# Interleaving the high and low parts of stationary matmul operands in a split-precision transformer kernel

## The chip, the cores and the metric

The kernel runs on one core of one Trainium2 chip. The metric is the device time of one execution in microseconds. Before the change three runs took 1825.13 us in the median, from 1824.33 to 1829.41. TensorE multiplies matrices, VectorE and ScalarE work element by element, GpSimd does some element work, and SyncE starts almost all DMA transfers.

## The reference

A small network of four layers is applied to 256 tokens of 1024 channels (and, in the first layer, to 256 context tokens besides). What matters here is that nearly all of its time goes into products of activations with weights:

```python
ql = pl[..., :D] ...                       # pl = u_lat @ w          (attention projections)
y_lat = swa(...) @ swa_wo[j]
h_lat = h_lat + ga2 * squared_relu_mlp(..., mlp_w1[i], mlp_w2[i])   # 1024 -> 4096 -> 1024
u = (xn @ w_in)                            # state-space mixer, then gelu(y) @ w_glu
val, gate = split(xn @ w_up); (silu(conv(gate)) * val) @ w_down     # 1024 -> 2 x 2816 -> 1024
```

Layer 0 attends in a neighbourhood, layer 1 in a sliding window, then come a state-space mixer with a gated MLP and a stick-breaking attention with another gated MLP. All is in 32-bit floating point.

## The kernel before

**Products of three terms.** TensorE multiplies the type float32r several times faster than float32, but keeps fewer bits. The kernel therefore writes each operand as high + low, both float32r, and makes each product of three: high x high, high x low, low x high. Every matmul has a stationary operand (`lhsT`, 128 columns, loaded ahead of it) and a moving one (`rhs`, 256 or 512 columns here). There are two forms.

- `mm_w` (lines 290 to 296): channels on the output's partitions, weights stationary, activations moving. Used for output projections, MLPs and the gated unit.
- `mm_x` (lines 298 to 304): tokens on the output's partitions, activations stationary, weights moving, 256 columns. Used for queries, keys, values and the input of the state-space mixer. A weight of 256 columns takes eight contraction tiles by four token tiles in layer 0 (12 such weights) and for the keys and values of layer 1 (2), and by two elsewhere (4 + 4 + 12): 14 x 32 + 20 x 16 = 768 of each of the three lines.

```python
294     T.matmul(ps, lhsT=a, rhs=xh[k][:, s0:s1], start=first, stop=False)       # mm_w: a, b = high, low weights
295     T.matmul(ps, lhsT=a, rhs=xl[k][:, s0:s1], start=False, stop=False)
296     T.matmul(ps, lhsT=b, rhs=xh[k][:, s0:s1], start=False, stop=last_)
302     T.matmul(ps, lhsT=xh[k][:, t0:t0 + 128], rhs=a, start=first, stop=False) # mm_x
303     T.matmul(ps, lhsT=xh[k][:, t0:t0 + 128], rhs=b, start=False, stop=False)
304     T.matmul(ps, lhsT=xl[k][:, t0:t0 + 128], rhs=a, start=False, stop=last_)
```

**Weights** (class `Weights`, lines 244 to 280). A part of at most 1024 elements per partition, that is eight column tiles of 128, comes by DMA from SyncE's queue into a `raw` tile. `split` (line 228) then makes `whi` with ScalarE (line 111, a copy that rounds) and `wlo` with VectorE (line 114, raw - whi). Each has its own tile of [128, 1024] from a pool of four buffers (line 862), and of five from layer 1's end on (line 1405): `wtile` (line 234) hands them out in turn. With `by_k`, used for `mm_x`, a part holds half the contraction with all 256 columns; without it, used for `mm_w`, one column tile of 128 with the whole contraction (or half of it). In `mm_w` a part of eight column tiles feeds 24 matmuls. With 512 tokens these stream 512 columns, with 256 tokens 256. The gated MLP opens two parts at a time, 48 matmuls of 256 columns.

**Activations.** `new_x` (line 486) makes tiles `xh0..7` and `xl0..7`, [128, 512] in the layers 0 and 1 and [128, 256] later; `normed` (line 470) and `gained` (line 465) fill them, high with ScalarE and low with VectorE. Hidden values and attention outputs lie in tiles `oh0..7` and `ol0..7` of another pool, [128, 512], made with the same function; the mixer's output `gh`, `gl` lies in four of each and moves in the 16 x 8 = 128 products per line of the gated unit. The state-space mixer takes its tokens in another order (`turned`, line 1452): there the elements of one instruction are written 128 bytes apart.

**The order of the work.** The program order is written out by hand. SyncE's queue starts loads in that order, each as soon as its buffer is free. In the attention stages `run_chains` (line 848) mixes scores, softmax and weighted sums of earlier heads with the projections of the next ones. Elsewhere products follow one another without a break, and each column tile's result is taken out of PSUM by VectorE or ScalarE while the next is made.

**Other users of the same memory.** While the program starts, the memory of `xh`, `xl` holds input rows and half tiles of conditioning weights (`stage`, line 872: 512 columns each). During the state-space mixer, `spare_w` (line 1428) lends idle `whi` and `wlo` tiles, in turns, to matrices that come back from DRAM.

Of the kernel before, what the change touches and what calls it, by code (L numbers as in the profile page):

```python
# [8 lines left out]
F32 = mybir.dt.float32  # L9
F32R = mybir.dt.float32r  # L10
# [7 lines left out]
KT = 8  # L18
# [67 lines left out]
def _build(ctx, tc, I, out, dbg):  # L86
# [10 lines left out]
    last = [None]  # L97
# [74 lines left out]
    def vector_loads(va, cc):  # L172
        """loads of the small vectors, most urgent first."""
# [58 lines left out]
    wpool, n_w = [], {}  # L232

    def wtile(tag, name, dt=F32R):
        i = n_w[tag] = n_w.get(tag, -1) + 1
        n = sum(b for _, b in wpool)
        p = wpool[0][0] if i % n < wpool[0][1] else wpool[1][0]
        return p.tile([128, 1024], dt, tag=tag, name=name)

    def w_pool(name, bufs):  # L240
        wpool.append((ctx.enter_context(tc.tile_pool(name=name, bufs=bufs)), bufs))
        n_w.clear()

    class Weights:
        """src: dram view [128, kt, n] or [128, kt, n / 128, 128]; parts of at most 1024 elements."""

        def __init__(self, src, by_k=False):
# [8 lines left out]
            for k0, k1, c0, c1 in spans:  # L256
# [12 lines left out]
                hi = wtile("whi", "whi")[:, 0:m]  # L269
                lo = wtile("wlo", "wlo")[:, 0:m]  # L270
# [14 lines left out]
    def wpairs(w, s, c0):  # L285
        """two column tiles of 128, one in each of two neighbouring blocks of s columns."""
        b = w.rearrange("(k p) (b n) -> p k b n", p=128, n=s)
        return b[:, :, c0 // s:c0 // s + 2, c0 % s:c0 % s + 128]

    def mm_w(ps, w, c0, x, k, s0, s1, first, last_):  # L290
        """channel-major product, one contraction tile: weights stationary."""
# [6 lines left out]
    def mm_x(ps, w, c0, c1, x, k, t0, first, last_):  # L298
        """token-major product, one contraction tile: activations stationary."""
# [6 lines left out]
    def gemm_w(tiles, x, nk, s0, s1, evac, lead):  # L306
        """tiles: list of callables giving (weights, column, psum view, key); the first `lead` of them go
        through the contraction together, so that they can start before all of x is there."""
# [10 lines left out]
    class Early:  # L319
        """the first two column tiles of a product, begun while its last contraction tiles are still missing."""  # L320
# [78 lines left out]
    def square_sum(n, pooled, view=lambda v: v, late=KT - 2):  # L399
        """tiles whose columns sum, over the partitions, to those of h * h."""  # L400
# [20 lines left out]
    def rstd_rows(n, pooled=6, late=KT - 2):  # L421
        """1 / rms of every token, a quarter of them on each block of 32 partitions."""
# [19 lines left out]
    def rstd(n, pooled=6, late=KT - 2, tag="x"):  # L442
        """1 / rms of every token, on all partitions; left in PSUM."""
        return spread_cols(rstd_rows(n, pooled, late), n, tag)

    def rstd_cols(view=lambda v: v, pooled=6):
        """1 / rms of every token, tokens on partitions: [128, 2]; view gives the order of the tokens."""
# [11 lines left out]
    def gained(x, gain, view=lambda v: v):  # L459
        """x = gain * h, for products that are scaled by the tokens' 1 / rms afterwards."""  # L460
# [5 lines left out]
    def normed(x, r, n, gain, shift=None):  # L466
        """gain(k, v), shift(k, v): columns for contraction tile k and stream v."""
# [15 lines left out]
    def new_x(pool, tag, n):  # L483
        return [[pool.tile([128, n], F32R, tag=f"{tag}{p}{k}", name=f"{tag}{p}{k}") for k in range(KT)]
                for p in "hl"]
# [7 lines left out]
    def rsqrt(y, ss, n, pool):  # L493
        """y = 1 / sqrt(ss / 64 + eps), by a bit estimate and three Newton steps."""
# [10 lines left out]
    def head_scale(views, pool, scale=(None, None)):  # L505
        """1 / rms of every head of token-major products [128, 256] in PSUM, times a scale of the tokens."""
# [11 lines left out]
    def head_norm(views, pool, scale=(None, None)):  # L518
        """per-head normalisation of token-major products [128, 256]; views in PSUM."""
# [10 lines left out]
    def stack_q(o, q):  # L530
        """heads of q, token-major [128, n, 64], as blocks (high, low) of 128 columns."""
# [3 lines left out]
    def stack_k(oh, ol, k):  # L535
        """heads of k as blocks (high, high) and (low, low): with those of q, two products make the whole q k."""
# [12 lines left out]
    def cmul(o, a, b, t, conj=False, e=None):  # L549
        """o = a * b (pairs of real and imaginary views); conj: a * conj(b)."""  # L550
# [41 lines left out]
    class S5:  # L592
        """operators of the state space layer: e = a^s b, k = c a^t b, f = c a^t, and the phases of a^8t."""

        def __init__(self, pp, loads):
# [43 lines left out]
            # input matrix: ((a - 1) / lam) * b  # L639
# [32 lines left out]
        def c(self):  # L672
            pp, ct, ci, dr = self.pp, self.ct, self.ci, self.dr
            # output matrix, transposed: states onto partitions
# [101 lines left out]
        def phases(self, fp, hf):  # L776
            """powers 1..32 of exp(8 i theta), and |a|^8 with a zero where a new group starts."""
# [21 lines left out]
        def f(self, fp, i):  # L799
            """state-to-output matrices, a sixteenth of the groups: real(c a s) needs (re, -im) of c a."""  # L800
# [17 lines left out]
    def softmax_rows(ps, n, at, idn, tail=None):  # L818
        """rows of ps [128, n] -> unnormalised weights and idn scaled by the rows' 1/sum."""
# [28 lines left out]
    def run_chains(chains, lag):  # L848
        """chains: list of (score, probs, [finish of a group]); every group is two chains long.
        score() -> state, probs(state) -> transposed weights, finish([both])."""  # L850
# [13 lines left out]
    # ================ start ================  # L864
    w_pool("wsp", 4)
    with ExitStack() as sa:
# [5 lines left out]
        def stage(p, i):  # L872
# [957 lines left out]
```

## Time and profile before

| what | value |
|---|---|
| median of three runs | 1825.13 us (1824.33 to 1829.41) |
| span of the profiled execution | 1823.7 us |
| matmuls / weight loads (TensorE) | 95% / 84% of the span |
| VectorE, ScalarE, GpSimd | 65%, 43%, 26% |
| DMA engines, mean share | 52% |
| bytes moved | 286.68 MB |
| granted TensorE clock, mean | 0.980 |

The profiled execution's own time is given by its span, from the first to the last instruction; what lies around it isn't listed apart, and the span is 1.4 us below the median. How to read it: the busy share of TensorE is a modelled one, since matmuls overlap, and what a matmul costs in a row of them is the distance of their starts. In names such as `g<-xh,whi` the output comes first, then the moving operand, then the stationary one. PE stands for matmuls, PEld for loads of the stationary operand, DVE for VectorE, ACT for ScalarE, SP for SyncE. A clock of 1.00 is 2.4 GHz.

### The profile page before, as it was taken

Reading aid. Unit: us, or ns where it says so; the run is one execution under the profiler, and the core shown is the slowest. Engines: PE = TensorE matmul, PEld = TensorE weight load, DVE = VectorE, ACT = ScalarE, POOL = GpSimd, SP = SyncE. Lnnn points to the kernel's source line nnn. Section 1 sums busy time; section 2 is a strip of 40 time slices with the busy share of each in tenths; the row PEclk is TensorE's granted clock in tenths of the full one; section 3 lists DMA queues with packets and bytes.
Section 4 is the critical chain, followed back from the end, with each engine's and each line's share of the span. In section 5 each row is a group of like instructions: output and inputs, shape, how many; then the busy total and the mean of one; then the engine's idle time right before and its main releaser. Section 6 shows DMA issues by size and latency. Waiting matters only on the chain. (4 is left out here: it accounts for less than half of the span.)

```text
span 1823.7 us, 34377 instructions
## 1 busy us (share of the span) xinstructions
PE 1738.8 (95%) x13449; PEld 1537.9 (84%) x13449; DVE 1183.4 (65%) x2508; ACT 790.0 (43%) x1446; POOL 473.1 (26%) x633
## 2 busy tenths in 40 slices
PE   5899999999999999999999999998999999999999
PEld 3478888877777777888878999987899999889998
DVE  8556776775635434346986656768576788958674
ACT  4344444442413222223654545545444465535453
POOL 5311211115789300030102000202331332324130
PEclk8899999999999999999999999998999999999999
DMA  8565454325566655332215566688558564435852
GB/s 221 172 175 155 147 173 122 106 86 162 170 212 219 184 170 162 93 93 81 59 36 146 155 189 186 193 303 235 142 153 231 152 218 131 127 93 167 228 156 88
DMA packets 441045, 286.68 MB, mean 157 GB/s; under 512 B 50450, under 2 KB 418610, under 8 KB 440882
## 3 DMA queue, kind: packets, MB, share of 16 engines
q1 hardware_dynamic: 439122, 278.70, 52.4%
q0 software_dynamic: 1760, 5.77, 0.8%
q8 instruction: 106, 1.74, 0.4%
q14 instruction: 57, 0.47, 0.1%
HBM read 271.48 MB, written 17.15 MB: 158 GB/s over the span
## 5 line engine op out<-in xcount | busy, mean ns | idle before, releaser
L111 ACT ACTIVATE whi<-raw 128x1024 fp32r<-128x1024 f32 (+2 forms) x388 | 389.8, 1013 | 482.2 <-PE g L295 352.3
L114 DVE TENSOR_TENSOR wlo<-raw,whi 128x1024 fp32r<-128x1024 f32 (+2 forms) x388 | 466.4, 1207 | 189.8 <-ACT whi L111 186.7
L296 PE MATMUL g<-xh,wlo 128*128 128x256 f32 (+1 forms) x1216 | 375.2, 309 | 5.5 <-DVE wlo L114 5.2
L294 PE MATMUL g<-xh,whi 128*128 128x256 f32 (+1 forms) x1216 | 375.2, 310 | 1.3 <-ACT xh L111 1.2
L295 PE MATMUL g<-xl,whi 128*128 128x256 f32 (+1 forms) x1216 | 374.6, 308 | 0.0
L294 PE MATMUL g<-oh,whi 128*128 128x256 f32 (+1 forms) x1056 | 332.1, 315 | 3.3 <-DVE hc L117 1.4
L296 PE MATMUL g<-oh,wlo 128*128 128x256 f32 (+1 forms) x1056 | 331.0, 314 | 0.0
L295 PE MATMUL g<-ol,whi 128*128 128x256 f32 (+1 forms) x1056 | 330.8, 313 | 0.0
L296 PEld LDWEIGHTS g<-xh,wlo 128*128 128x128 f32 x1216 | 235.2, 193 | 17.9 <-DVE wlo L114 7.4
L294 PEld LDWEIGHTS g<-xh,whi 128*128 128x128 f32 x1216 | 234.7, 193 | 16.4 <-ACT whi L111 3.1
L295 PEld LDWEIGHTS g<-xl,whi 128*128 128x128 f32 x1216 | 235.3, 193 | 9.7
L294 PEld LDWEIGHTS g<-oh,whi 128*128 128x128 f32 x1056 | 198.3, 188 | 23.6 <-issue 3.9
L295 PEld LDWEIGHTS g<-ol,whi 128*128 128x128 f32 x1056 | 198.3, 188 | 15.3 <-issue 1.1
L296 PEld LDWEIGHTS g<-oh,wlo 128*128 128x128 f32 x1056 | 198.3, 188 | 14.5 <-issue 0.2
L302 PE MATMUL g<-whi,xh 128*128 128x256 f32 x560 | 166.9, 298 | 3.8 <-ACT xh L111 2.8
L303 PE MATMUL g<-wlo,xh 128*128 128x256 f32 x560 | 161.1, 288 | 0.6 <-DVE wlo L114 0.6
L304 PE MATMUL g<-whi,xl 128*128 128x256 f32 x560 | 160.5, 288 | 0.1
L117 DVE SCALAR_TENSOR_TENSOR h<-g,mods,h 128x256 f32<-128x256 f32 x64 | 30.8, 482 | 141.5 <-PE g L296 141.5
L302 PEld LDWEIGHTS g<-whi,xh 128*128 128x128 f32 x560 | 108.6, 194 | 13.3 <-issue 8.5
L303 PEld LDWEIGHTS g<-wlo,xh 128*128 128x128 f32 x560 | 108.8, 194 | 2.2 <-DVE wlo L114 1.7
L304 PEld LDWEIGHTS g<-whi,xl 128*128 128x128 f32 x560 | 108.1, 194 | 0.5 <-DVE xl L117 0.3
L111 ACT ACTIVATE oh<-t 128x256 fp32r<-128x256 f32 (+1 forms) x108 | 51.3, 482 | 125.5 <-DVE t L114 125.5
(300 smaller groups left out, 2943.3 us busy)
## 6 DMA issues: line engine op xcount, KB each, us to landing
raw<-mlp_w SPq DMA_DIRECT2D x128, 512.0 KB, 4.6
ada<-ada_w SPq DMA_DIRECT2D x88, 512.0 KB, 5.4
raw<-ffn_w_up SPq DMA_DIRECT2D x88, 512.0 KB, 5.2
raw<-ffn_w_down SPq DMA_DIRECT2D x32, 384.0 KB, 3.6
raw<-ffn_w_down SPq DMA_DIRECT2D x32, 320.0 KB
raw<-na_wqkv SPq DMA_DIRECT2D x32, 256.0 KB, 4.4
raw<-a_w_glu SPq DMA_DIRECT2D x16, 512.0 KB, 7.9
raw<-w_kv SPq DMA_DIRECT2D x16, 512.0 KB, 4.5
```

What stands on the lines that cost most here:

```text
L111: last[0] = A.activation(out=o, in_=i, func=f, **kw)
L114: (e or V).tensor_tensor(out=o, in0=a, in1=b, op=op)
L117: V.scalar_tensor_tensor(out=o, in0=a, scalar=s, in1=b, op0=op0, op1=op1)
L294: T.matmul(ps, lhsT=a, rhs=xh[k][:, s0:s1], start=first, stop=False)
L295: T.matmul(ps, lhsT=a, rhs=xl[k][:, s0:s1], start=False, stop=False)
L296: T.matmul(ps, lhsT=b, rhs=xh[k][:, s0:s1], start=False, stop=last_)
L302: T.matmul(ps, lhsT=xh[k][:, t0:t0 + 128], rhs=a, start=first, stop=False)
L303: T.matmul(ps, lhsT=xh[k][:, t0:t0 + 128], rhs=b, start=False, stop=False)
L304: T.matmul(ps, lhsT=xl[k][:, t0:t0 + 128], rhs=a, start=False, stop=last_)
```

## The change

The high and low parts of an operand now share one tile. Where the operand is stationary they are interleaved, element by element: high at even places, low at odd ones, so that each is read and written with a step of two elements (eight bytes). Where it moves, they lie one after the other, each contiguous. Weights are paired unless `by_k`; activations are paired where `mm_x` uses them (`True` below) and not where `mm_w` does. Tiles `oh`, `ol`, `gh`, `gl` stay as they were. The weight pool hands out tiles of [128, 2048], the same number of them, and the staging and spare tiles follow: staging tiles are 1024 wide, so the conditioning weights that went into two half tiles come with one DMA each, and two spare tiles are the halves of one.

```diff
-    def wtile(tag, name, dt=F32R):
-        i = n_w[tag] = n_w.get(tag, -1) + 1
-        n = sum(b for _, b in wpool)
-        p = wpool[0][0] if i % n < wpool[0][1] else wpool[1][0]
-        return p.tile([128, 1024], dt, tag=tag, name=name)
+    def wtile(name, dt=F32R):
+        n_w[0] += 1
+        p = wpool[0][0] if n_w[0] % sum(b for _, b in wpool) < wpool[0][1] else wpool[1][0]
+        return p.tile([128, 2048], dt, tag="w", name=name)
...
+    def two(t, n, paired):
+
+        if paired:
+            v = t.rearrange("p (n c) -> p c n", c=2)
+            return v[:, 0, 0:n], v[:, 1, 0:n]
+        return t[:, 0:n], t[:, n:2 * n]
...
-                hi = wtile("whi", "whi")[:, 0:m]
-                lo = wtile("wlo", "wlo")[:, 0:m]
+                hi, lo = two(wtile("w")[:, 0:2 * m], m, not by_k)
                 split(hi, lo, r)
...
-    def new_x(pool, tag, n):
-        return [[pool.tile([128, n], F32R, tag=f"{tag}{p}{k}", name=f"{tag}{p}{k}") for k in range(KT)]
-                for p in "hl"]
+    def new_o():
+        return [[actp.tile([128, 512], F32R, tag=f"o{p}{k}", name=f"o{p}{k}") for k in range(KT)] for p in "hl"]
+
+    def new_x(pool, tag, n, paired):
+
+        return list(zip(*[two(pool.tile([128, 2 * n], F32R, tag=f"{tag}{k}", name=f"{tag}{k}"), n, paired)
+                          for k in range(KT)]))
...
-        def stage(p, i):
-            return xa.tile([128, 512], F32, tag=f"x{p}{i}", name=f"st{p}{i}")
-
+        def stage(i):
+            return xa.tile([128, 1024], F32, tag=f"x{i}", name=f"st{i}")
...
-            halves = lambda k: [stage("l", 2 * (k // 2) + j) for j in range(2)] if k % 2 else None
+            halves = lambda k: [stage(4 + k // 2)] if k % 2 else None
...
-            x = new_x(xa, "x", 512)
+            x = new_x(xa, "x", 512, True)
...
-            x = new_x(xa, "x", 512)
+            x = new_x(xa, "x", 512, False)
             mod_norm(x, 0, 3, 512)
...
+        halves = []
+
         def spare_w():
-            """tiles of the pool of weight parts, which idles meanwhile."""
-            return wtile("whi" if n_w["whi"] == n_w["wlo"] else "wlo", "sw", F32)
+
+            if not halves:
+                t = wtile("sw", F32)
+                halves.extend((t[:, 1024:2048], t[:, 0:1024]))
+            return halves.pop()
...
-        x = new_x(xb, "x", 256)
+        x = new_x(xb, "x", 256, True)
         turned = lambda v: v.rearrange("p (t c) -> p c t", t=8)
...
-        x_ = new_x(xb, "x", 256)
+        x_ = new_x(xb, "x", 256, False)
...
-        xk = new_x(xb, "x", 256)
-        xq = new_x(ac, "xq", 256)
+        xk = new_x(xb, "x", 256, True)
+        xq = new_x(ac, "xq", 256, True)
```

The matmuls of lines 294 to 296 and 302 to 304 are not edited; only the views that they get are others. The rest of the diff takes comments away or passes the new arguments on.

## Rows read from the trace of the kernel before

**Rows 1.** The page, part 1: busy us, share of the span, instructions.

```profile
PE 1738.8 (95%) x13449; PEld 1537.9 (84%) x13449; DVE 1183.4 (65%) x2508; ACT 790.0 (43%) x1446; POOL 473.1 (26%) x633
```

**Rows 2.** Waits: us in total, times, longest us.

```profile
ACT whi L111 <- PE g L295: 352.3, 153, 8.7
...
PE g L296 <- DVE wlo L114: 5.8, 7, 1.9
```

**Rows 3.** Timeline of PE (start us, us), first and last of four unbroken sequences.

```profile
1439.76 0.28 PE L296 MATMUL g<-xh,wlo 128*128 128x256 f32 x1
...
1441.92 0.28 PE L296 MATMUL g<-xh,wlo 128*128 128x256 f32 x1
...
1081.79 0.28 PE L294 MATMUL g<-oh,whi 128*128 128x256 f32 x1
...
1083.83 0.28 PE L294 MATMUL g<-oh,whi 128*128 128x256 f32 x1
...
469.64 0.39 PE L296 MATMUL g<-xh,wlo 128*128 128x512 f32 x1
...
471.68 0.39 PE L296 MATMUL g<-xh,wlo 128*128 128x512 f32 x1
...
411.80 0.39 PE L296 MATMUL g<-oh,wlo 128*128 128x512 f32 x1
...
413.89 0.39 PE L296 MATMUL g<-oh,wlo 128*128 128x512 f32 x1
```

**Rows 4.** Windows, gated MLP: us; PE, PEld, DVE, ACT, POOL busy; PEclk, DMA share, GB/s.

```profile
1400.00:1455.00 55.00, 55.00 (x460) 55.00 (x459) 41.20 (x66) 26.16 (x37) 19.02 (x19) 1.00 0.59 169
```

**Rows 5.** Timeline of the weight loads (PEld).

```profile
1439.76 0.19 PEld L294 LDWEIGHTS g<-xh,whi 128*128 128x128 f32 x1
```

**Rows 6.** Lines, shapes apart: busy us, mean ns, idle before; L294, L302.

```profile
L294 PE MATMUL g<-xh,whi 128*128 128x256 f32 x960 | 274.6, 287 | 1.2 <-ACT xh L111 1.2
...
L294 PE MATMUL g<-oh,whi 128*128 128x256 f32 x736 | 204.0, 278 | 1.2 <-DVE h L117 0.7 <-ACT oh L111 0.5
...
L302 PE MATMUL g<-whi,xh 128*128 128x256 f32 x560 | 166.9, 298 | 3.8 <-ACT xh L111 2.8 <-DVE h L114 1.0
...
L294 PE MATMUL g<-oh,whi 128*128 128x512 f32 x320 | 128.1, 401 | 2.1 <-DVE hc L117 1.4 <-ACT oh L111 0.7
...
L294 PE MATMUL g<-xh,whi 128*128 128x512 f32 x256 | 100.6, 395 | 0.1
```

**Rows 7.** Timeline of PE, float32 products (two passes each).

```profile
145.82 1.05 PE L839 MATMUL pt<-dg,p 128*128 128x128 f32 x8
...
1550.87 0.60 PE L1721 MATMUL z<-kT,qz 128*128 128x256 f32 x2
1551.30 0.27 PE L1742 MATMUL pt<-cst,be 128*128 128x128 f32 x1
```

**Rows 8.** Splits by shape, then wider steps: ACT's in the timeline, DVE's by shape.

```profile
L111 ACT ACTIVATE whi<-raw 128x1024 fp32r<-128x1024 f32 x324 | 340.4, 1057 | 451.7 <-PE g L295 325.0 <-issue 38.5 <-PE g L304 34.3
...
L114 DVE TENSOR_TENSOR wlo<-raw,whi 128x1024 fp32r<-128x1024 f32 x324 | 409.8, 1268 | 172.1 <-ACT whi L111 169.1
...
1153.11 0.78 ACT L111 ACTIVATE xh<-h,vt 128x256 fp32r<-128x256 f32 x1
...
1280.34 0.51 ACT L111 ACTIVATE xh<-h,vt 128x256 fp32r<-128x256 f32 x1
...
L114 DVE TENSOR_TENSOR gl<-x,gh 128x128 fp32r<-128x128 f32 x16 | 6.0, 396 | 2.6 <-ACT gh L111 2.6
...
L114 DVE TENSOR_TENSOR qn<-g,ri 128x128 f32<-128x128 f32 x32 | 8.9, 279 | 0.0
```

**Rows 9.** Waits of PE for the staged conditioning weights.

```profile
PE x L360 <- DMA stl<-ada_w: 1.1, 1, 1.1
```

**Rows 10.** Timeline of PE, float32r transposes of 128 columns.

```profile
299.92 0.23 PE L1013 MATMUL pt<-idr,sp 128*128 128x128 f32 x1
...
300.39 0.62 PE L1013 MATMUL pt<-idr,sp 128*128 128x128 f32 x6
```

More of the change, by code (lines that the diff above doesn't have):

```diff
@@ L230, in split @@
         tt(o_lo, x, o_hi.bitcast(F32), SUB)
-    wpool, n_w = [], {}
-    def wtile(tag, name, dt=F32R):
-        i = n_w[tag] = n_w.get(tag, -1) + 1
-        n = sum(b for _, b in wpool)
-        p = wpool[0][0] if i % n < wpool[0][1] else wpool[1][0]
-        return p.tile([128, 1024], dt, tag=tag, name=name)
+    wpool, n_w = [], [-1]
+    def wtile(name, dt=F32R):
+        n_w[0] += 1
+        p = wpool[0][0] if n_w[0] % sum(b for _, b in wpool) < wpool[0][1] else wpool[1][0]
+        return p.tile([128, 2048], dt, tag="w", name=name)
     def w_pool(name, bufs):
         wpool.append((ctx.enter_context(tc.tile_pool(name=name, bufs=bufs)), bufs))
-        n_w.clear()
+        n_w[0] = -1
+    def two(t, n, paired):
[3 more added lines that the diff above has]
+        return t[:, 0:n], t[:, n:2 * n]
     class Weights:
@@ L894, in _build @@
                 for t in range(2):
-                    r = [stage("h", len(xt) * 2 + j) for j in range(2)]
+                    r = stage(len(xt))
                     for j in range(2):
                         xloads.append(lambda r=r, nm=nm, t=t, j=j: dma(
-                            out=r[j], in_=I[nm][0, t * 128:(t + 1) * 128, 512 * j:512 * j + 512]))
+                            out=r[:, 512 * j:512 * j + 512],
+                            in_=I[nm][0, t * 128:(t + 1) * 128, 512 * j:512 * j + 512]))
                     xt.append(r)
-            halves = lambda k: [stage("l", 2 * (k // 2) + j) for j in range(2)] if k % 2 else None
+            halves = lambda k: [stage(4 + k // 2)] if k % 2 else None
             ada_q = ada_steps(0, 0, halves) + ada_steps(0, 1, halves)
@@ L920, in _build @@
                 for t in range(4):
-                    T.transpose(ps[:, t * 128:(t + 1) * 128], xt[t][k // 4][:, (k % 4) * 128:(k % 4) * 128 + 128], ident)
+                    T.transpose(ps[:, t * 128:(t + 1) * 128], xt[t][:, k * 128:k * 128 + 128], ident)
                 act(h[k], ps[:, 0:256], AF.Copy)
@@ L1159, in mlp @@
         def mlp(l, ntok, x_, after=None):
-            hid = new_x(actp, "o", 512)
+            hid = new_o()
             per = 512 // ntok
@@ L1200, in _build @@
             dump("h0", 512)
-            x = new_x(xa, "x", 512)
+            x = new_x(xa, "x", 512, True)
             mod_norm(x, 1, 0, 512)
             mark("norm1")
-        oT = new_x(actp, "o", 512)
+        oT = new_o()
         with ExitStack() as s0:
@@ L1375, in _build @@
             rawp[0] = ctx.enter_context(tc.tile_pool(name="rawb", bufs=8, side="right"))
-            x = new_x(xa, "x", 512)
+            x = new_x(xa, "x", 512, False)
             mod_norm(x, 1, 3, 256)
@@ L1610, in scales @@
                 act(rb, spread_cols(sd[0], 256)[:, 0:256], AF.Copy)
-        hid = new_x(actp, "o", 512)
+        hid = new_o()
         hv = [[t[:, j * 256:(j + 1) * 256] for t in hx for j in range(2)] for hx in hid]
@@ L1650, in _build @@
         mark("norm2")
-        oT = new_x(actp, "o", 512)
+        oT = new_o()
         wkv, wq = I["w_kv_2"], I["b_w_q_2"][0]
```

## The prediction

> **What bounds the kernel now.** I read the busy shares first: TensorE's matmuls cover 95% of the span, VectorE 65%, ScalarE 43% [rows 1]. Then the waits: ScalarE, which makes the high part of every weight, waits 352 us in total for matmuls to free its buffers, while TensorE waits 5.8 us in total for the low parts that VectorE makes [rows 2]. So the weight pipeline runs ahead and TensorE sets the time. The question is thus what one matmul costs, and that is read from starts, since matmuls overlap and their durations are modelled. In the timeline of TensorE, 18 products of 256 columns with tile x moving take 2.16 us, 120 ns each; 18 with tile o moving take 2.04 us, 113.3 ns each; with 512 columns, 9 take 2.04 us (x, 226.7 ns) and 9 take 2.09 us (o, 232.2 ns) [rows 3]. The reader should see two things. First, 256 more columns of x cost 226.7 - 120 = 106.7 ns, one column per tick at 2.4 GHz (the granted clock is 1.00 in such a stretch [rows 4]); so 120 ns is a stream of 106.7 and 13.3 ns lost, and 113.3 loses 6.6. Second, line and shape are the same in both 256-column cases and only the moving tile differs, so what is lost depends on where operands lie. The next product's load starts together with a matmul, at 1439.76 both [rows 3, 5], so both reads run side by side.
>
> **The change, part by part.**
> (a) Every stationary operand of lines 294 to 296 (weights) and 302 to 304 (activations) is read with a step of two elements. Nothing is added or removed on TensorE: 9504 matmuls keep count, order and shape. By the groups [rows 6] they are: x moving, 256 columns, 960 x 3 = 2880 at 120 ns; the token-major ones, 768 x 3 = 2304 by the loops (560 per line write tile g), also at 120; o moving, 256 columns, 736 x 3, with the gated unit's 128 x 3 together 2592 at 113.3; 512 columns, x 256 x 3 = 768 at 226.7 and o 320 x 3 = 960 at 232.2. No product in this trace has a strided stationary operand, so the new pace is bounded. The nearest rows are fp32 products, in which the stream advances at half speed: two passes of 256 columns take 0.43 us, 215 ns each, and eight passes of 128 columns (1.05 - 0.27) / 7 = 111 ns [rows 7], though each passes 107 ns of stream and loads 128 fresh stationary columns. There stream and load step through memory at the same rate and only 4 to 5 ns are lost; in the products at hand the moving stream goes by two elements where, in the same time, the load need take one. My theory is that the loss is the two reads meeting again and again because one overtakes the other, and that a load stepping by two elements keeps abreast. Then 256 columns cost 111 ns and 512 cost 216. That is an inference from the fp32 rows; it isn't shown.
> Sum at full effect: 2880 x 9 = 25.9; 2304 x 9 = 20.7; 2592 x 2.3 = 6.0; 768 x 10.7 = 8.2; 960 x 16.2 = 15.6; together 76 us. The token-major products feed attention, whose chains wait for VectorE and GpSimd as well; I let half of their 20.7 land. Of the other 55.7 I let nine tenths land, as the starts of stages (norms) don't shrink: 10.4 + 50.1 = 60 us. Ends: all loss gone, 5184 x 13.3 + 2592 x 6.6 + 768 x 13.3 + 960 x 18.8 = 114 us of gain; or, if the strided load meets the stream oftener, a loss (rival 2). I take the value near the fp32 rows, since there the same widths are read in the same time.
> The trace says that the pace of one shape moves by 6.7 ns with the moving tile [rows 3]. The Trainium skill (TensorE: Matmul & The Clock Gate, Step-by-step: what each phase is for) says that the stationary and the moving operand have independent read ports, so that a load takes no bandwidth from a running matmul; by it the layout of weights changes nothing and this sum is 0. It is rival 1.
> (b) The splits write with a step of two elements: ScalarE 1057 ns and VectorE 1268 ns per part of 1024 [rows 8]. The 2400 high column tiles of lines 294 to 296 make 300 paired parts of eight. The trace has wider steps only: ScalarE's 256 elements written 128 bytes apart take 0.78 us against 0.51, and VectorE's 128 written 32 bytes apart 396 ns against 279 [rows 8], 0.9 to 1.05 ns more per element. So a part costs between 0 and 0.93 us more on VectorE. I take 0: eight bytes is nearest to the contiguous row. The cover is VectorE's idle quarter: 41.2 us busy of 55 in the densest stretch [rows 4]; rival 3 is what happens if it goes.
> The Trainium skill (Advanced Engine Details and Errata, SBUF Cachelines) wants two accesses per 16-byte line for full speed, which a step of two fp32 keeps; by it (b) is 0 too. No row here has that step.
> (c) High and low parts share a tile, so a buffer is freed after the third product of its last group, not the second: 0.12 us later, hidden, because the split is four buffers ahead [rows 2]. If the first product must now wait for the low part too, that is 1.27 us at each start of a stage that has no part ready, about ten; TensorE's present 5.8 us of such waits is the nearest row, and I count 0 to 6 as within the error.
> (d) The staging tiles double in width: SyncE issues 8 loads of 512 KB instead of 16 of 256 KB. TensorE waits 1.1 us for them now [rows 9], so -1 to +1; I take 0. The spare tiles of the state-space stage come in pairs that are freed together, so that a transfer into the first half may start later by the use of the second; I take 0.
> So: the span is 1823.7, 1.4 below the median of 1825.1; from that median, 1825 - 60 = **1765 us**.
>
> **Rivals.**
> 1. Nothing changes: the loss is TensorE's own per instruction and independent of the load's layout. For it: 13.3 ns is lost at 256 and at 512 columns of x alike. Against: 113 and 120 for one shape. Time: 1820 to 1830.
> 2. Slower: the strided load touches twice as much memory, and meets the moving stream twice as often. Its place is each of the 9504 matmuls; its price is the present loss again, 2880 x 13.3 + 2304 x 13.3 / 2 + 2592 x 6.6 + 768 x 13.3 + 960 x 18.8 = 99 us: 1924 us; with half of it 1875. It decides as soon as a 256-column product of x starts more than 120 ns after the one before. For it: six 128-column transposes of the same type take (0.62 - 0.23) / 5 = 78 ns apiece [rows 10], over the 53 of their stream, so a load isn't free even now; were it to double, 156 ns would bind everywhere at 256 columns, 5184 x 36 + 2592 x 43 = 298 us more, 2123 us. Against: the fp32 rows.
> 3. The splits become the bound: strided writes cost 0.93 us per part on VectorE. In the gated MLP two parts are split per 5.76 us of TensorE (48 products), and VectorE goes from 41.2 of 55 us to 41.2 + 19 x 0.93 = 58.9 (19 parts in 55 us), 7% over. The 44 pairs' 253 us grow by 18. With no gain elsewhere that is 1843 us; with the gain of (a) outside it, 1765 + 18 + 19 (the 88 x 24 products of that stage, 9 ns each) = 1802, within the forecast's own range.
>
> **How the numbers follow.** Forecast 0.58, rival 1 0.14, rival 2 0.20, rival 3 without a gain 0.08. Forecast first, as its rows are the nearest in kind; rival 2 has a real row for it. The forecast's own range is 1730 (all but a few us of the 114 lands) to 1805. To leave out no more than 2 in 10, the range goes over rivals 1 and 3 and up to the half-sized rival 2: 1730 to 1885. A measurement tells 0.3%, 5.5 us, from no change: faster 0.58, within 0.14, slower 0.28.
>
> **What would show it.** Right: in the timeline of the gated MLP, 256-column products start 109 to 113 ns apart whichever tile moves, and 512-column ones 215 to 219; durations of the splits stay at 1.06 and 1.27 us; VectorE still waits for ScalarE and ScalarE for TensorE. Step (a) is wrong if the 120 stays (rival 1) or grows (rival 2); (b) is wrong if the split's mean rises towards 2 us and TensorE's waits for low parts leave single figures. If the pace falls and the time doesn't, another engine or the DMA queues took over, and the waits will name it.

## The result and the profile after

The changed kernel is slower: 1859.8 us in the median of four runs (1856.7 to 1863.6) against 1827.3 (1824.3 to 1829.7) for the kernel before, a ratio of 1.0174 with an interval of 1.0154 to 1.0194. Forecast were 1765 us. The profiled execution of the changed kernel has a span of 1855.0 us.

Busy shares of the changed kernel, the page's part 1, to be read against [rows 1]:

```profile
PE 1764.1 (95%) x13449; PEld 1570.8 (85%) x13449; DVE 1183.2 (64%) x2508; ACT 812.9 (44%) x1446; POOL 446.5 (24%) x633
```

The shape is the same: as many instructions on each engine, TensorE at 95%. ScalarE is busy 22.9 us longer and VectorE not at all. The lines of the splits, shapes apart (busy us, mean ns, idle before), say why:

```profile
L111 ACT ACTIVATE w<-raw 128x1024 fp32r<-128x1024 f32 x324 | 365.4, 1133 | 353.3 <-PE g L302 236.8 <-PE g L310 34.5 <-issue 34.1
...
L114 DVE TENSOR_TENSOR w<-raw,w 128x1024 fp32r<-128x1024 f32 x324 | 412.3, 1276 | 113.6 <-ACT w L111 112.5 <-DMA vt<-vdr 0.7
```

Against [rows 8], the means rise by 76 ns per part on ScalarE (1133 for 1057) and by 8 ns on VectorE (1276 for 1268). But these groups mix two kinds: 68 of the 324 parts are `by_k`, which the change leaves contiguous, and in the trace 68 of ScalarE's still take 1059 ns. The 256 interleaved ones take 1153, so a step of two costs ScalarE 96 ns per part.

The pace comes next. These are the first and the last start of the same four kinds of sequence as in [rows 3], in the changed kernel's timeline of TensorE: 18 products of 256 columns with x and with o moving, 9 of 512 columns with x and with o.

```profile
1425.12 0.28 PE L300 MATMUL g<-x,w 128*128 128x256 f32 x1
...
1427.28 0.28 PE L300 MATMUL g<-x,w 128*128 128x256 f32 x1
...
1075.04 0.28 PE L300 MATMUL g<-oh,w 128*128 128x256 f32 x1
...
1077.20 0.28 PE L300 MATMUL g<-oh,w 128*128 128x256 f32 x1
...
465.21 0.39 PE L300 MATMUL g<-x,w 128*128 128x512 f32 x1
...
467.31 0.39 PE L300 MATMUL g<-x,w 128*128 128x512 f32 x1
...
425.11 0.39 PE L300 MATMUL g<-oh,w 128*128 128x512 f32 x1
...
427.17 0.39 PE L300 MATMUL g<-oh,w 128*128 128x512 f32 x1
```

That is 120.0, 120.0, 233.3 and 229 ns where the kernel before had 120.0, 113.3, 226.7 and 232.2. Nothing got below 120 at 256 columns: x stayed, o lost 6.7 ns, and 512 columns of x lost 6.6. Over all starts of the two traces (pairs under 127 ns at 256 columns and under 241 at 512, so that gaps stay out) the means are:

| products | in rows (after) | before | after | sum |
|---|---|---|---|---|
| 256 columns, o or g moving | 2527 | 113.7 ns | 120.0 ns | +16.0 us |
| 512 columns, x moving | 737 | 227.7 | 233.2 | +4.1 |
| 512 columns, o moving | 902 | 233.3 | 231.3 | -1.8 |
| 256 columns, x moving | 2757 | 119.9 | 120.0 | +0.1 |
| token-major | 2006 | 119.6 | 120.0 | +0.8 |

So 19 of the 31 us between the spans lie in the pace. Of the rest, 9 lie in gaps between products with x moving at 256 columns, and 3 between TensorE's other matmuls. In the changed kernel's waits (us in total, times, longest us) the waits of TensorE for low parts, 5.8 us before [rows 2], have doubled, and there are some for high parts too:

```profile
ACT w L111 <- PE g L302: 263.3, 111, 8.0
...
PE g L302 <- DVE w L114: 11.0, 15, 1.9
...
PE g L300 <- ACT w L111: 2.4, 5, 0.9
```

They fall in the gated MLPs, as here in the timeline of TensorE:

```profile
1467.24 0.39 PE L300 MATMUL g<-x,w 128*128 128x256 f32 x1 [0.45 <-ACT w L111]
...
1468.64 0.39 PE L302 MATMUL g<-x,w 128*128 128x256 f32 x1 [0.89 <-DVE w L114]
```

Why parts come late there is seen on VectorE. First one column tile of the kernel before, then one of the changed kernel, both from the timeline of VectorE in a gated MLP (t<-gp is a step of the convolution, t<-t,g the product of gate and value, wlo or w the low split):

```profile
1437.88 0.48 DVE L117 SCALAR_TENSOR_TENSOR t<-gp,vt,t 128x256 f32<-128x256 f32 x1 [0.47 <-POOL t L124]
1438.28 1.22 DVE L114 TENSOR_TENSOR wlo<-raw,whi 128x1024 fp32r<-128x1024 f32 x1
1439.41 0.48 DVE L117 SCALAR_TENSOR_TENSOR t<-gp,vt,t 128x256 f32<-128x256 f32 x1
1439.97 1.23 DVE L114 TENSOR_TENSOR wlo<-raw,whi 128x1024 fp32r<-128x1024 f32 x1
1441.84 0.42 DVE L114 TENSOR_TENSOR t<-t,g 128x256 f32<-128x256 f32 x1 [0.64 <-POOL t L114]
```

```profile
1454.27 0.42 DVE L114 TENSOR_TENSOR t<-t,g 128x256 f32<-128x256 f32 x1 [1.38 <-POOL t L114]
1454.61 1.22 DVE L114 TENSOR_TENSOR w<-raw,w 128x1024 fp32r<-128x1024 f32 x1
...
1457.26 0.48 DVE L117 SCALAR_TENSOR_TENSOR t<-gp,vt,t 128x256 f32<-128x256 f32 x1 [0.77 <-POOL t L124]
1457.66 1.22 DVE L114 TENSOR_TENSOR w<-raw,w 128x1024 fp32r<-128x1024 f32 x1
1458.80 0.48 DVE L117 SCALAR_TENSOR_TENSOR t<-gp,vt,t 128x256 f32<-128x256 f32 x1
```

Before, both splits stand ahead of the product, and the second fills the time in which ScalarE and GpSimd prepare it. After, the second split stands behind the product: VectorE idles 1.38 us for GpSimd, and then splits while the next column tile's chain waits. No instruction of this chain was edited, and yet the order differs between the two traces. That a tile with both parts comes free for the next weight at another moment than two tiles did, and that the order follows from it when the program is built, is the likely reason; it wasn't shown. The period follows from ScalarE's timeline (the activation of the gate), first in the kernel before, then in the changed one:

```profile
1434.22 0.42 ACT L111 ACTIVATE t<-t 128x256 f32<-128x256 f32 x1
...
1439.98 0.42 ACT L111 ACTIVATE t<-t 128x256 f32<-128x256 f32 x1
```

```profile
1452.98 0.42 ACT L111 ACTIVATE t<-t 128x256 f32<-128x256 f32 x1 [3.17 <-DVE t L117]
...
1459.37 0.42 ACT L111 ACTIVATE t<-t 128x256 f32<-128x256 f32 x1 [3.17 <-DVE t L117]
```

Before, a column tile took 5.76 us, which is TensorE's 48 x 120. Now it takes this chain 6.39 us, and TensorE 5.76 as before. The splits are ahead by the pool's buffers, lose 0.6 us of that lead per column tile, and after a number of tiles TensorE waits.

### The profile page after: what moved, and what is told of

It is laid out like the page before. It is cut to its first block, busy times and chain, and to the rows that moved or that the text cites. A ratio compares the mean times of both kernels' runs of the same rounds, so it can differ in the third digit from the quotient of the medians.

```text
span 1855.0 us, 34335 instructions
## 1 busy us (share of the span) xinstructions
PE 1764.1 (95%) x13449; PEld 1570.8 (85%) x13449; DVE 1183.2 (64%) x2508; ACT 812.9 (44%) x1446; POOL 446.5 (24%) x633
## 3 DMA queue, kind: packets, MB, share of 16 engines
q8 instruction: 106, 1.74, 0.4%
## 4 chain that ended last, share of the span: by engine, by line
PE 63%; DVE 9%; issue 4%; POOL 3%; ACT 2%; DMA 1%; POOLq 0%; ACTq 0%; SPq 0%; DVEq 0%
PE g L300 16%; PE g L302 16%; PE g L301 16%; DVE w L114 3%; PE pt L849 2%; PE g L308 2%; PE g L309 2%; PE g L310 2%; POOL t L114 1%; PE x L366 1%; POOL t L124 1%; PE po L1344 1%; DVE t L117 1%; PE sc L1334 1%; ACT t L111 1%
## 5 line engine op out<-in xcount | busy, mean ns | idle before, releaser
L111 ACT ACTIVATE w<-raw 128x1024 fp32r<-128x1024 f32 (+2 forms) x388 | 419.3, 1087 | 383.8 <-PE g L302 263.3
L114 DVE TENSOR_TENSOR w<-raw,w 128x1024 fp32r<-128x1024 f32 (+2 forms) x388 | 469.2, 1213 | 132.8 <-ACT w L111 131.5
L302 PE MATMUL g<-x,w 128*128 128x256 f32 (+1 forms) x1216 | 376.9, 310 | 9.5 <-DVE w L114 9.5
L300 PE MATMUL g<-x,w 128*128 128x256 f32 (+1 forms) x1216 | 376.6, 311 | 3.6 <-ACT w L111 2.4
L301 PE MATMUL g<-x,w 128*128 128x256 f32 (+1 forms) x1216 | 375.6, 309 | 0.0
L300 PE MATMUL g<-oh,w 128*128 128x256 f32 (+1 forms) x1056 | 336.9, 320 | 3.0 <-ACT oh L111 1.2
L301 PE MATMUL g<-ol,w 128*128 128x256 f32 (+1 forms) x1056 | 335.3, 318 | 0.0
L302 PE MATMUL g<-oh,w 128*128 128x256 f32 (+1 forms) x1056 | 333.9, 316 | 0.5 <-DVE w L114 0.5
L302 PEld LDWEIGHTS g<-x,w 128*128 128x128 f32 x1216 | 240.0, 197 | 22.3 <-DVE w L114 12.1
L300 PEld LDWEIGHTS g<-x,w 128*128 128x128 f32 x1216 | 239.5, 197 | 19.3 <-ACT w L111 3.4
L301 PEld LDWEIGHTS g<-x,w 128*128 128x128 f32 x1216 | 240.0, 197 | 10.1 <-DVE t L117 0.4
L300 PEld LDWEIGHTS g<-oh,w 128*128 128x128 f32 x1056 | 205.2, 195 | 20.8 <-issue 6.0
L302 PEld LDWEIGHTS g<-oh,w 128*128 128x128 f32 x1056 | 206.2, 195 | 12.4 <-DVE w L114 0.7
L301 PEld LDWEIGHTS g<-ol,w 128*128 128x128 f32 x1056 | 205.1, 194 | 12.3 <-issue 1.1
L308 PE MATMUL g<-w,x 128*128 128x256 f32 x560 | 167.6, 300 | 3.4 <-ACT x L111 2.8
L309 PE MATMUL g<-w,x 128*128 128x256 f32 x560 | 161.4, 289 | 0.3 <-DVE w L114 0.3
L310 PE MATMUL g<-w,x 128*128 128x256 f32 x560 | 160.7, 288 | 0.0
L308 PEld LDWEIGHTS g<-w,x 128*128 128x128 f32 x560 | 111.2, 199 | 12.7 <-issue 7.2
L309 PEld LDWEIGHTS g<-w,x 128*128 128x128 f32 x560 | 111.3, 199 | 1.6 <-DVE w L114 1.1
L310 PEld LDWEIGHTS g<-w,x 128*128 128x128 f32 x560 | 110.9, 199 | 0.3
```

The source lines that it names most:

```text
L111: last[0] = A.activation(out=o, in_=i, func=f, **kw)
L114: (e or V).tensor_tensor(out=o, in0=a, in1=b, op=op)
```

## The experiments

Three candidates were to be told apart: the step of two in the stationary operand, the sharing of a tile (with the order that comes of it), and the strided writes of the splits.

**e1_merged: the sharing without the interleaving.**

```diff
     def two(t, n, paired):
-
-        if paired:
-            v = t.rearrange("p (n c) -> p c n", c=2)
-            return v[:, 0, 0:n], v[:, 1, 0:n]
         return t[:, 0:n], t[:, n:2 * n]
```

> The changed kernel with high and low parts in one tile as in the change, but never interleaved: each part is contiguous, nothing else differs. Theory 'the step': reading the stationary operand with a step of two elements is what slows the products. Then 256-column products with o moving go back from 120.0 to 113.7 ns (2548 of them in rows, 16.1 us), 512-column ones with x moving from 233.2 to 227.7 (738, 4.1 us), those with o moving from 231.3 up to 233.3 (903, -1.8 us), the token-major ones from 120.0 to 119.6 (0.8 us): about 19 us less than the changed kernel, 1840 us; the gaps of the gated MLPs stay. Rival 'the sharing': one tile for both parts does all of it, since parts lie elsewhere in memory and come free together; then 1860 us and a pace of 120.0 stay. Rival 'the writing': the splits' strided writes delay the parts; then ScalarE's split falls from 1133 to 1057 ns, the gaps of the gated MLPs go as well, and the time is that of the kernel before, 1827 us.

Measured: 1839.2 us (1835.9 to 1842.3), 1.0053 times the kernel before (1.0036 to 1.0070). The timeline of TensorE, o and then x:

```profile
1075.01 0.28 PE L299 MATMUL g<-oh,w 128*128 128x256 f32 x1
...
1077.05 0.28 PE L299 MATMUL g<-oh,w 128*128 128x256 f32 x1
...
465.23 0.39 PE L298 MATMUL g<-x,w 128*128 128x512 f32 x1
...
467.27 0.39 PE L298 MATMUL g<-x,w 128*128 128x512 f32 x1
```

113.3 and 226.7 ns again. The waits for low parts stay:

```profile
PE g L299 <- DVE w L114: 12.2, 15, 1.9
```

So the step owns the loss of pace, and the sharing the gaps; the writing owns neither, since ScalarE's split fell to 1056 ns here and the gaps did not go. Nothing else is mixed in: the traces of the two runs have the same order of instructions on TensorE, VectorE and ScalarE, and a column tile of the gated MLPs takes 6.38 us here too.

**e2_ordered: the changed kernel, asked for VectorE's order of before.** Weights are opened three column tiles ahead in the text, and the product is issued behind the low split of the farthest. These are two edits at once.

```diff
+                if behind:
+                    upto(i + 4)
+                evac(m, pa, pb, *([ws[cols[i + 3]].lows[0] if i + 3 < len(cols) else None] if behind else []))
...
-            tt(c1[:, 0:256], c1[:, 256:512], pv_, MUL)
+            with tc.issue_after(late.ins) if late else ExitStack():
+                tt(c1[:, 0:256], c1[:, 256:512], pv_, MUL)
```

> The changed kernel, interleaved, with one more edge in the gated MLPs: the product of the activated gate with the value is issued behind the low split of a part three column tiles ahead, so that VectorE's instructions stand in the order of the kernel before (two splits between the convolution's steps and that product). Theory 'the order': sharing a tile moved a split behind that product, the chain of one column tile grew to 6.39 us against TensorE's 5.76 us, the lead of the weight pipeline is used up and TensorE stalls for about 10 us in the two gated MLPs. Then the period of a column tile on VectorE returns to 5.76 us, TensorE's waits for low parts fall from 11.0 to about 6 us, and the time is 1848 to 1851 us, while the pace of products stays at 120.0 ns. Rival 'the release': a part that is freed one product later is what stalls it, whatever the order; then the waits and 1860 us stay.

Measured: 1848.8 us (1844.1 to 1851.8), 1.0097 (1.0080 to 1.0114). The waits:

```profile
PE g L305 <- DVE w L232: 6.8, 10, 1.9
```

Time and waits came as the order would have it: 11 us less than the changed kernel. The period did not: ScalarE's activations of the gate lie 5.6 to 6.6 us apart, some 6.1 in the mean, and VectorE's order is that of before only in part: in some column tiles it still waits 1.59 us, for ScalarE's high part. That still uses up lead, but little of it shows: the waits are 1 us above those of the kernel before. The rival 'the release' is out. Whether the new order won the time, or the earlier opening of the weights, this run doesn't tell.

**e4_merged_ordered: both edits together.**

> The contiguous shared tiles of the run e1_merged with the order of the run e2_ordered in the gated MLPs: of the change only the sharing itself is left. If the step and the order are all that the change costs, the two gains add: 1859.8 - 20.6 - 11.1 = 1828 us, within 4 us of the kernel before, and TensorE's gaps with x moving fall from 35 to about 26 us. If something else of the sharing costs (the later release of a part, the double staging tiles), it stays between 1832 and 1840 us.

Measured: 1833.3 us (1830.0 to 1837.3), 1.0022 (1.0009 to 1.0035). Waits for low parts:

```profile
PE g L302 <- DVE w L232: 7.2, 10, 1.9
```

This leaves 0.2%, some 4 us, to the rest of the sharing. Its cause was not looked for; the order on VectorE and ScalarE differs from that of before in other stages too. So the 1.74% of the change are made of 0.22 (rest of the sharing), 0.31 (what the edits of e2_ordered win back, e1_merged less e4_merged_ordered) and 1.21 (the step, the changed kernel less e1_merged). Taken the other way round, those edits win 0.77 (1.0174 less 1.0097) and the step costs 0.75. The two ways differ by hardly more than the four intervals allow, and in both pairs of traces TensorE's gaps between products shrink by the same 6 us, so a dearer order together with the step isn't shown. The 18 us of pace, 1.0%, lie between the two values for the step.

**e9_acts: activations interleaved, weights contiguous.**

```diff
-                hi, lo = two(wtile("w")[:, 0:2 * m], m, not by_k)
+                hi, lo = two(wtile("w")[:, 0:2 * m], m, False)
```

> The changed kernel with activations interleaved as in the change, weights shared but contiguous: one of its two interleavings alone. By the traces so far the token-major products cost 119.6 ns each contiguous and 120.0 interleaved (0.8 us in all), so this is the run e1_merged to within the measurement: 1839 to 1841 us; the 20 us belong to the weights. Rival: writing activations with a step (ScalarE's and VectorE's 256-element splits) delays the starts of stages; then 1845 us or more.

Measured: 1840.9 us (1837.2 to 1841.3), 1.0077 (1.0060 to 1.0093). By the medians that is e1_merged; by the ratios 0.2% more, and the intervals overlap. Most of the step's loss belongs to the weights: 0.97 of 1.21 by the ratios, and all but 1 us of the pace.

**e3_pace: products alone.** The kernel holds rows of 48 products and nothing of the network; its output is zeros, and so it is in e7_pace2 and e8_load. Here a and b are high and low parts in the stationary tile, with a step of one or two, and xh and xl lie in the moving tile, which is shifted:

```python
T.matmul(ps, lhsT=a, rhs=xh, start=r == 0 and k == 0, stop=False)
T.matmul(ps, lhsT=a, rhs=xl, start=False, stop=False)
T.matmul(ps, lhsT=b, rhs=xh, start=False, stop=r == reps - 1 and k == KT - 1)
```

> Only products, none of the network: rows of 48 matmuls in the pattern high-high, high-low, low-high over eight contraction tiles, from one tile of stationary and one of moving elements, with nothing else running. For a step of one and of two elements in the stationary operand, and for 256 and 512 moving columns, the start of the moving tile is shifted by 0, 16, 32, 64, 128, 192, 256, 320, 384 and 448 bytes against the stationary one. Theory 'the step': with a step of one the 256-column pace depends on the shift, 120 ns at 0 and 113 ns at others (448 among them, where tile o lay); with a step of two it is 120 ns or more at every shift, and 512 columns take 231 to 234. Rival 'the place': a step of two has its good shifts too, at 113 ns or less, and the change only met bad ones. Rival 'independent reads': 120 at every shift and step, and what made 113 in the kernel lies elsewhere. 64 and 128 columns show what a load alone allows: if a load of step two is the longer one, its pace there is above that of step one.

The timeline of TensorE, 42 products at a shift of 448 bytes, first at step one and then at step two:

```profile
84.74 0.28 PE L51 MATMUL one_half_j<-x,w 128*128 128x256 f32 x1
...
89.50 0.28 PE L51 MATMUL one_half_j<-x,w 128*128 128x256 f32 x1
...
270.01 0.29 PE L51 MATMUL two_half_j<-x,w 128*128 128x256 f32 x1
...
275.06 0.28 PE L51 MATMUL two_half_j<-x,w 128*128 128x256 f32 x1
```

113.3 against 120.2 ns, with no other engine at work. Medians of all rows, ns:

```
shift, bytes      0   16   32   64  128  192  256  320  384  448
256 col, step 1  120  118  117  118  119  118  120  118  119  113
256 col, step 2  120  119  120  120  120  120  120  120  120  121
512 col, step 1  227  230  234  229  232  232  227  229  232  233
512 col, step 2  233  232  233  232  231  229  233  232  232  230
```

At step one the place decides, between 113 and 120 and between 227 and 234; at step two 256 columns take 119 to 121 wherever they lie. 'The step' was a little off: 16 bytes came to 119, and 512 columns to 229 to 233 where 231 to 234 were expected. Neither independent reads nor a good place for step two is left. In the kernel before, o lies at 448 bytes against the weights (counted to multiples of 512) and x at 0. This is worked out from the sizes of its tiles; no trace lists addresses, but the paces fit: the best place for 256 columns (o), the best for 512 (x), and close to the worst for each the other way round. Step two gave up the two good ones and had little to gain at the bad ones.

**e7_pace2: larger steps, and a finer sweep.**

> Only products again, in the pattern of the run e3_pace: a stationary step of 1, 2, 4 and 8 elements at a shift of 0 and of 448 bytes; then a moving step of 2 against a stationary step of 1 and 2; then step one at every multiple of 16 bytes up to 496, with 256 and 512 columns. Theory 'spread': with any step above one the loss no longer depends on the place and stays near 13 ns at 256 columns (120 ns) up to a step of 8. Rival 'more memory, more meetings': it grows with the step, 133 ns or more at 4. Theory of the prediction ('abreast'): a moving step of two against a stationary one of two is like one against one, and two against one is worse. In the sweep the best places for 256 columns are expected between 432 and 464 bytes, at 113 ns, and none below 111.

Steps 1, 2, 4 and 8 took 113.7, 120.1, 235.4 and 243.4 ns at 448 bytes. A moving operand with a step of two took 229 to 230 ns, whatever the stationary one did. The timeline at step four and shift 0, 42 products:

```profile
71.59 0.39 PE L53 MATMUL four_a<-x,w 128*128 128x256 f32 x1
...
81.39 0.39 PE L53 MATMUL four_a<-x,w 128*128 128x256 f32 x1
```

'Spread' missed (step four costs 113 ns more, not nothing); 'more memory, more meetings' has the direction, but not that step two costs 0 to 6 ns and step four doubles the time; 'abreast' is refuted, since moving by two costs a whole stream at either stationary step. In the sweep 113 ns came at 64, 112, 192, 368 and 448 bytes, not around 448 alone, and none was below. One place can have two paces, though; 64 and 320 bytes differ by a whole 256 and still, 42 products each:

```profile
183.60 0.28 PE L53 MATMUL half_ae<-x,w 128*128 128x256 f32 x1
...
188.36 0.28 PE L53 MATMUL half_ae<-x,w 128*128 128x256 f32 x1
...
273.98 0.28 PE L53 MATMUL half_ce<-x,w 128*128 128x256 f32 x1
...
278.92 0.28 PE L53 MATMUL half_ce<-x,w 128*128 128x256 f32 x1
```

113.3 and 117.6 ns; in e3_pace 64 bytes had 118. What chooses between them stays open.

**e8_load: how long a load takes.** Rows of few columns, each behind products of 512 columns that keep the clock up.

> Only products. How long a load of the stationary operand takes by itself: rows of 24 products of 64, 128, 192 and 256 moving columns, with a stationary step of 1, 2, 3 and 4 elements, each row behind 48 products of 512 columns. Where the moving columns pass faster than the load, the pace is the load's. Theory 'the load is the bound': at step one 64, 128 and 192 columns all take about 112 ns, though their columns pass in 27, 53 and 80; at step two about 118; at step four about 233, whatever the width. So at 256 columns (106.7 ns of stream) the load is the longer of the two at either step, and step two adds its 6 ns wherever the place had not lost them already. Rival 'meetings only': the pace follows the columns (30, 60, 90 ns) at steps one and two, so that a load costs only where it meets the stream.

The timeline of TensorE, 18 products each: 128 columns at the steps one, two and four, then 64 at step two.

```profile
112.42 0.28 PE L53 MATMUL one_quarter<-x,w 128*128 128x128 f32 x1
...
114.43 0.28 PE L53 MATMUL one_quarter<-x,w 128*128 128x128 f32 x1
...
126.07 0.28 PE L53 MATMUL two_quarter<-x,w 128*128 128x128 f32 x1
...
128.19 0.28 PE L53 MATMUL two_quarter<-x,w 128*128 128x128 f32 x1
...
156.89 0.40 PE L53 MATMUL four_quarter<-x,w 128*128 128x128 f32 x1
...
161.10 0.43 PE L53 MATMUL four_quarter<-x,w 128*128 128x128 f32 x1
...
62.50 0.28 PE L53 MATMUL two_sixty<-x,w 128*128 128x64 f32 x1
...
64.62 0.28 PE L53 MATMUL two_sixty<-x,w 128*128 128x64 f32 x1
```

111.7, 117.8 and 233.9 ns, and 117.8 for half the columns: the pace is the load's, not the stream's (53 and 27 ns). Step three took 173 to 175. 192 columns gave 111.8 and 118.7. The row of 64 columns at step one came out ahead of the rows that were to keep the clock up, took 213 ns and says nothing; e3_pace has 112 for it at a granted clock of 0.98. 'Meetings only' is out. So a load takes longer than 256 columns of stream (106.7 ns), and a step of two makes it 6 ns longer.

The Trainium skill (TensorE: Matmul & The Clock Gate, LDWEIGHTS (loading the stationary operand)) gives a load its number of columns over 1.2, in ns, an estimate of 107 for 128 columns. The runs come within 5 ns of it, with 111.7 at step one and a granted clock of 1.00.

**e5_place and e6_place2: the kernel before, with its tiles elsewhere.** Nothing interleaved, nothing shared; the traces show the order of before on TensorE, VectorE and ScalarE.

```diff
     xb = ctx.enter_context(tc.tile_pool(name="xb", bufs=1))
+    G.memset(xb.tile([128, 112], F32, name="shift"), 0.0)
+    gap = ctx.enter_context(tc.tile_pool(name="gap", bufs=1))
+    G.memset(gap.tile([128, 16], F32, name="gap"), 0.0)
     w_pool("wsq", 1)
```

In e6_place2 there is one line more:

```diff
         xa = sa.enter_context(tc.tile_pool(name="xa", bufs=1))
+        G.memset(xa.tile([128, 16], F32, name="shift"), 0.0)
```

> The kernel before, in which the tiles x of the last three layers lie 448 bytes further (64 less than a multiple of 512), so that moving x stands to stationary weights as tile o does; the weights stay where they were against 512. Nothing is interleaved or shared. Theory 'the place' (contiguous operands lose by where they lie): the 2112 products of the two gated MLPs with x moving go from 119.9 to 113.7 ns, 13.1 us, and the token-major products of these layers, which then stand 64 bytes the other way, from 120 to about 118, 1 us or less: 1829.9 - 14 = 1816 us. Rival 'another bound': the gated MLP's period of 5.76 us per column tile is set by VectorE and ScalarE as well; then starts are 113 ns apart but gaps come between column tiles, and the time stays at 1826 to 1830 us.

> The run e5_place, and in addition the tiles x of the layers 0 and 1 lie 64 bytes further, so that moving weights stand 64 bytes below stationary x. Theory 'the place': the 1344 token-major products of these layers go from 120 to 114 ns, 8 us, of which half lands, since attention waits for VectorE too; 512-column products with x moving go from 227.7 to 228.8 (0.9 us lost), the 768 products of 256 columns of layer 1's MLP from 119.9 to 118 (1.5 us won): about 5 us less than e5_place, 1811 us. Rival: only the difference to a multiple of 512 in the moving tile's own address counts, not that between the two; then the token-major products stay at 120 ns and the time is that of e5_place.

Measured: e5_place 1820.4 us (1817.5 to 1824.0), 0.9955 (0.9942 to 0.9968); e6_place2 1820.2 us (1817.0 to 1823.6), 0.9952 (0.9937 to 0.9966). Both are faster than both kernels, by 8 us where 14 and 19 were expected. The timeline and a wait of e5_place:

```profile
1425.02 0.28 PE L295 MATMUL g<-xl,whi 128*128 128x256 f32 x1
...
1427.06 0.28 PE L295 MATMUL g<-xl,whi 128*128 128x256 f32 x1
```

```profile
PE g L296 <- DVE wlo L114: 8.8, 10, 1.9
```

In the first gated MLP x now runs at 113.3 ns (114.3 in the mean), so the place does what it was to do. What is missing from the 14 us lies in the pace: in the last gated MLP it is 117 ns at the same addresses, the second pace that e7_pace2 shows, and o slides to 118 in part of it. Over the whole trace the pace gives 9 us less, and TensorE's gaps between products stay as they were. 'Another bound' was right in that the chain of a column tile now sets the period in the first gated MLP, 5.57 us against 48 x 113.3 = 5.44, and TensorE's waits for low parts rise from 5.8 to 8.8 us; but it costs little. In e6_place2, where the stationary tile moved, the token-major products of the layers 0 and 1 fell to 116.2 and 114.0 ns. In e3_pace the moving tile moved; so it is the distance between the two that counts. In turn o and half of x slid to 118 ns in the first gated MLP, with no address changed against e5_place. That took some 5 us, as much as the token-major products had won. The gaps of the profiled execution are 7 us longer besides; their cause was not looked for.

## Why the prediction was wrong

The measured 1859.8 us lie within the range (1730 to 1885), on the side that got 0.28.

**What bounds the kernel:** right. In the kernel before TensorE set the time, the pace is to be read from starts, and it depends on where operands lie; e3_pace and e5_place bear it out.

**Step (a) failed**, and at one sentence: that the load need take one element in the time in which the moving stream takes two, so that a load "stepping by two elements keeps abreast". The load has no time to spare. It is itself longer than the stream: 111.7 ns for 128 columns against 106.7 for 256. The 111 ns of the fp32 rows [rows 7], which I took for a stream of 107 with 4 to 5 ns lost, is within 1 ns of the time of that load (whether the load sets it there too wasn't tried). The row that should have stopped me is [rows 10]: there 128 columns cost 78 ns over a stream of 53, so something longer than the stream set the pace. I put it down under a rival. (Products load slower still, 111.7; why transposes take less wasn't tried.) With the load as the bound, a step of two can only add, 6 ns here, and 256 columns can't come below 118. Forecast were 76 us of gain for the pace at full effect; it cost 19. This account doesn't reach the 512-column products: their stream of 213 ns is longer than either load, and still they take 227 to 234. What they lose there, and why the place counts at all, stays open.

**Rival 1** (0.14), that layout changes nothing, held for x at 256 columns and for the token-major products (119.9 and 119.6 to 120.0 ns), over half of all products, and failed for o. The rule that it stood on, read ports that do not disturb each other (the Trainium skill, TensorE: Matmul & The Clock Gate, Step-by-step: what each phase is for), does not agree with e3_pace: with nothing else running, shifting one operand alone moves the pace from 113 to 120 ns.

**Rival 2** (0.20) had the direction and the kind of cause, a strided load that costs more, but its price was mis-sized: the present loss again, 99 us, or 50 at half. What it costs at 256 columns is 6 ns of load, and that only where the place had not lost them already; with the 512-column products it comes to 19 us. Its alternative, a load that doubles, starts at a step of four (234 ns), not of two.

**Step (b)**: VectorE's 0 was right (8 ns per part). ScalarE's 96 ns per interleaved part were not foreseen. The gaps aren't theirs, since e1_merged writes without a step and still has them; what they cost besides is lost in the noise. **Rival 3** named the right place, VectorE in the gated MLP as the bound, by the wrong means. The Trainium skill (Advanced Engine Details and Errata, SBUF Cachelines) asks for two accesses per 16-byte line. For VectorE's writes the rows go its way: a step of two, which keeps two, costs 8 ns in 1276, and the step of 32 bytes in [rows 8], which leaves one, 0.9 ns per element, though the two rows compared there differ in their operands as well. For loads the runs come near to it: a step of two, which keeps two, costs 6 ns, and a step of four, which leaves one, doubles the time.

**Step (c)**, 0 to 6 us for the shared tile, was too low: e1_merged says 0.53%, some 10 us. The step failed where it counted only the wait of a later release; front and prediction both took the order of the work as written by hand. It is not: sharing moved a split behind another instruction on VectorE, and the "cover" that I named for the splits, VectorE's idle quarter, says nothing about a chain in which an engine waits in order. **Step (d)**: TensorE's waits for the conditioning weights are 1 us longer, as allowed for.

## What to carry to other kernels

Before changing the layout of an operand, measure how long the load alone takes, by products with too few columns to hide it; where it is as long as the stream, a step in the stationary operand can only lose: here a step of three took half as long again as step one, and a step of four twice as long. Where such a kernel loses a few per cent to products that start later than their columns allow, look at the distance between the two operands' addresses first: a pad of 512 bytes took 0.45% off here, with no instruction of the network changed. After a change that regroups buffers, compare the order of instructions on each engine before and after; it can move where the text didn't.

## What the runs showed that I had not expected

- The pace depends on the distance of moving and stationary operand (113 to 120 ns at 256 columns, 227 to 234 at 512), and the best place differs between the widths: 448 bytes is best for 256 columns and among the worst for 512.
- The same addresses can run at 113 or at 118 ns from one stage to another (e5_place, e6_place2, e7_pace2). It explains most of why 8 us came where 14 were expected, and its cause is open.
- A moving operand with a step of two takes twice the time (229 ns for 256 columns); a stationary one up to 6% more, and nothing more where the place had already lost it.
- In e3_pace TensorE's granted clock was 1.00 in rows of 512 columns and fell to 0.50, the lower of its levels (1.2 GHz), behind 5 us of 64-column products, though the engine never paused; 128 columns then took 213 ns. The windows of that run (us; PE and PEld busy, ACT, POOL, granted clock, DMA share, GB/s):

```profile
200.00:206.00 6.00, 6.00 (x53) 5.91 (x51) 0.00 (x0) 0.00 (x0) 0.98 0.00 0
206.00:216.00 10.00, 10.00 (x49) 10.00 (x48) 0.00 (x0) 0.00 (x0) 0.50 0.01 2
```
